# Mixers and norms of a hybrid encoder: sums of squares from split values, decay projection and meta keys on 128 rows, low parts of the gate weights on VectorE

## The chip, the cores and the metric

The kernel runs on one core of a Trainium2 chip. The metric is device time in microseconds (us) of one execution; three runs of the kernel before took 2300.5, 2293.67 and 2294.09, a median of 2294.09. The engines are called as in the profile: PE is TensorE's matmuls and PEld its weight loads, DVE is VectorE, ACT is ScalarE, POOL is GpSimd, SP is SyncE, which only issues transfers here.

## The reference, cut to what matters

A trunk of two layers works on 528 tokens (512 and 16 meta tokens) of 1024 channels, in float32. Each layer is half a feed-forward network, a mixer and another half feed-forward network, each behind an RMS norm.

```python
for l in range(2):
    h = h + 0.5 * swiglu(rmsnorm(h, g[l, 0]), ...)      # 1024 -> 2816 -> 1024
    h = h + mixer(rmsnorm(h, g[l, 1]), ...)
    h = h + 0.5 * swiglu(rmsnorm(h, g[l, 2]), ...)
out = rmsnorm(h, final_norm)[:, 16:]                    # without the meta tokens

rmsnorm(x, g) = x * rsqrt(mean(x * x) + 1e-6) * g

mixer(z):
    q_a, k_a, v_a, r_a, lr_f, lr_b, q_b, k_b, v_b, g_a, g_b = split(z @ w_in)
    a = gla_branch(...)         # 4 heads; decay = log_sigmoid(lr @ w2 + b2) / 16, lr of rank 16,
                                # one decay for each of two directions; heads normed, times silu(r_a)
    b = attention_branch(...)   # 8 query heads of 64, 2 key/value heads, q and k normed and rotated
    return (sigmoid(g_a + b0) * (a @ w_pa) + sigmoid(g_b + b1) * (b @ w_pb)) @ w_out
```

## The kernel before

Activations lie transposed: channels on the 128 partitions, tokens along the row, in two halves of 264 tokens. TensorE multiplies float32 in two ways. A plain float32 matmul passes over its rows several times. Everything large is split instead: a value is the sum of a high part, rounded to a faster type (fp32r in the profile) by a ScalarE copy, and a low part, the rest, by a VectorE subtraction; a product is then three fp32r matmuls, high by high, high by low and low by high (`product`, L374 to L383, the matmul in L382).

*Weights.* Slabs of 128x1024 arrive in the order of a plan, on SP's queue, up to six ahead (class `Weights`). `make` (L210 to L231) turns a slab into its two parts, up to four ahead: ScalarE casts it (`whi`, L222) and VectorE subtracts (`wlo`, L227). For the last twelve gate projections of a mixer, which TensorE works on beside attention, a flag `by_dma` chooses another way to the low part: ScalarE writes the negated high part (L224), and a transfer issued by GpSimd adds the slab to it (L225, by way of L178).

*Feed-forward networks* (L482 to L574) build seven products in place of eight by sums of weight blocks; their matmul is L502 and the change leaves them alone, but their norms are the `Norm` below.

*Norms.* `Norm` collects the squares of the channel chunks in a float32 tile (L414 to L420). `rs` (L458) has TensorE add them over the partitions, with a constant matrix of 1/1024 in float32 (`means`, L385 to L389), and `rsqrt_of` (L391) takes the root with a logarithm, an exponential and one correction step. The norms of the linear attention's heads (L735 to L737) and of the attention's keys (L759) use `means` with matrices of 1/128 and 1/64. The last norm stands in the tail (L1005 to L1025), in two column halves.

*The mixer* (L916 to L971) loads the decay weights `w2t` (33 rows: two times 16 ranks and a bias, L921), projects r, takes the norm's root, projects the low-rank values (`product` with 32 columns, L933; a row of ones is added, L935) and then runs `gla_pair` for two pairs of heads. In `gla_pair`, for each direction, L612 multiplies `w2t` with `lr` on 33 rows in float32, VectorE and ScalarE make the cumulated decays of it, and the keys times decay are transposed (L655). Then come the states of four blocks of 128 tokens and the meta tokens (L691 to L711), the scores (L718), and the outputs, from the scores (L727) and from the state (L728). A state has the forward direction on partitions 0 to 63 and the backward one on 64 to 127; block 3, the last, has no backward state and the meta block no forward one, so there L728 uses 64 rows.

*Attention* (L752 to L906). `probs` makes the softmax of 128 queries: two times two score matmuls, a maximum on VectorE, an exponential on ScalarE, a normalisation. `weighted` (L853 to L880) transposes the probabilities of two such blocks (L861), splits them, and multiplies them with the values. The values are stored as high part in 64 columns and low part in the next 64, so one matmul with the probabilities' high part (L878) and one with their low part (L879) give all products. The 16 meta keys come last, as a contraction over 16 rows of `vm` (L772) and `tail`. For each of the two key heads there are eight sums of 256 columns in each layer, and in layer 0 one of 64 columns for the meta tokens' own queries: 34 in all.

*The order.* The program is written for a scheduler that decides each engine's order from dependencies and priorities; `tc.high_priority` marks the work behind a norm's sum. Each engine then takes its instructions in that order. Tiles come from pools with a fixed number of buffers (six of `t`, one of `lr` in the mixer), and a write waits until the buffer's last reader is through.

```python
if self.by_dma:                                                                   # L223
    nc.scalar.activation(lo[:, cs], hi[:, cs].bitcast(F32), AF.Copy, scale=-1.0)  # L224
    self.add(lo[:, cs].bitcast(F32), w[:, cs])                                    # L225
else:
    nc.vector.tensor_tensor(lo[:, cs], w[:, cs], hi[:, cs].bitcast(F32), ALU.subtract)
```

Of the kernel before, what the change touches and what calls it, by code (L numbers as in the profile page):

```python
# [17 lines left out]
P = 128  # L18
D = 1024
# [8 lines left out]
EPS = 1e-6  # L28
NB = SEQ // P
# [107 lines left out]
C_O1024, C_O128, C_B64 = C_ID + P, C_ID + 2 * P, C_ID + 3 * P  # L137
C_DIAG = C_ID + 4 * P
NCONST = C_DIAG + P


class Weights:
# [3 lines left out]
    def __init__(self, nc, raw, hi, lo, wts, win):  # L146
        self.nc, self.raw, self.hi_pool, self.lo_pool, self.wts, self.win = nc, raw, hi, lo, wts, win
        self.long = self.short = None
        self.by_dma = False
# [59 lines left out]
    def make(self, upto):  # L209
        nc = self.nc  # L210
        while self.made < min(upto, len(self.loads)):
# [8 lines left out]
            for a in np.split(np.arange(SLAB), 2 if s == 0 else 1):  # L220
                cs = slice(a[0], a[-1] + 1)
                nc.scalar.copy(hi[:, cs], w[:, cs])  # L222
                if self.by_dma:  # L223
                    nc.scalar.activation(lo[:, cs], hi[:, cs].bitcast(F32), AF.Copy, scale=-1.0)  # L224
                    self.add(lo[:, cs].bitcast(F32), w[:, cs])  # L225
                else:
                    nc.vector.tensor_tensor(lo[:, cs], w[:, cs], hi[:, cs].bitcast(F32), ALU.subtract)  # L227
# [11 lines left out]
    def next(self, name):  # L239
# [5 lines left out]
        return hi[:, c : c + t[5]], lo[:, c : c + t[5]]  # L245

# [7 lines left out]
def build(tc, ctx, xt, wts, win, par, w2, const, umask, out):  # L254
# [70 lines left out]
    o1024, o128 = ct[:, C_O1024 : C_O1024 + P], ct[:, C_O128 : C_O128 + P]  # L325
# [59 lines left out]
    def means(weights, x):  # L385
        acc = Acc("ss", x.shape[-1])
        for a, hs in zip(acc.half, acc.spans):
            TE.matmul(a, weights, x[:, hs], start=True, stop=True)  # L388
        return acc  # L389

    def rsqrt_of(acc, y, newton):  # L391

        (ms, cut), = acc.parts
        S.activation(cut(y), ms, AF.Ln, bias=eps, scale=1.0)
        act(y, y, AF.Exp, scale=-0.5)
        if newton:
            u = slot("t", n=y.shape[-1])
            S.activation(u, y, AF.Square)
            V.scalar_tensor_tensor(cut(u), ms, EPS, cut(u), ALU.add, ALU.mult)
            V.scalar_tensor_tensor(y, u, 3.0, y, ALU.subtract, ALU.mult)  # L400

    class Norm:
# [55 lines left out]
        def rs(self):  # L458

            rs = slot("rs")  # L460
            with tc.high_priority():
                ms = means(o1024, self.acc)
                with after(table("natural_log_exp_and_others")):
                    rsqrt_of(ms, rs, True)
# [125 lines left out]
    def gla_pair(l, p, lr, w2t, sr, qa, ka, va, n_out):  # L590
# [17 lines left out]
        for d in range(2):  # L608
            z = pair()
            for i, hs in enumerate(halves):  # L610
                c0 = p * 256 + d * P
                TE.matmul(z[:, i, :HF], w2t[:33, c0 : c0 + P], lr[:33, hs], start=True, stop=True)  # L612
# [61 lines left out]
        st_m = slot("k")  # L674

# [34 lines left out]
        for b in [3, 2, 1, 0] + [NB] * (n_out == T):  # L710
# [383 lines left out]
```

## Time and profile before

| | before |
|---|---|
| three runs, us | 2293.67, 2294.09, 2300.5 |
| median, us | 2294.09 |
| the profiled execution's span, us | 2289.1 |
| weights and activations read | 264.38 MB, 116 GB/s over the span |
| L382, split products in the mixers, x6570 | 494.2 + 383.5 + 309.9 + 267.2 us busy in its four largest groups |
| L502, split products of the feed-forward networks, x7392 | 902.3 + 702.1 us busy |
| L227, low parts of weights on VectorE | 267.9 + 203.1 + 107.6 us busy |

The span is that of the profiled execution, from its first to its last instruction; the runs are timed without a profile. Busy time of TensorE is modelled from the start and the length of its matmuls: two that follow each other 0.12 us apart can each be recorded with 0.28 us, since a matmul's length holds the time until its result has left the array. What a matmul costs the queue is therefore read from start to start.

The page cuts the span into 40 slices of 57 us. Layer 0's mixer lies between some 390 and 806 us, layer 1's between some 1535 and 1930 us; TensorE is at 9 tenths or more in all slices but the first, the 21st and the last.

### The profile page before, as it was taken

The page shows a single profiled execution, that of the slowest core. Times are in us where ns is not written, and L with a number is a line of the kernel's source. Part 1 is how long each engine was busy: PE and PEld are TensorE (multiplying, and loading weights), DVE is VectorE, ACT ScalarE, POOL GpSimd, SP SyncE. Part 2 cuts the span into 40 slices and gives each one's busy share as a digit, 9 for nine tenths or more (in the row PEclk, how much of TensorE's full clock was granted, in tenths as well). Part 3 has the DMA queues.
Part 4 walks back from the last instruction along what each step waited for, and adds up shares of the span by engine and source line. Part 5 has one row for each costly group of instructions (what it writes and reads, how often), then busy time and mean ns, then how long its engine had stood idle before and what let it go on. Part 6 is the DMA issues. An engine that isn't in the chain of part 4 may idle for free.

```text
span 2289.1 us, 39919 instructions
## 1 busy us (share of the span) xinstructions
PE 2225.1 (97%) x16548; PEld 2108.4 (92%) x16548; DVE 1491.3 (65%) x2355; ACT 1214.4 (53%) x1785; POOL 195.1 (9%) x218
## 2 busy tenths in 40 slices
PE   5999999999999999999989999999999999999997
PEld 5999999989999999999989999998788888989896
DVE  6656567476775676565676565674768667756566
ACT  7536355344786564453565353553448946636452
POOL 1111010010000010101011110100000001101010
PEclk9999999999999999999989999999999999999999
DMA  8858562211325485766667585632113356859661
GB/s 225 236 150 224 142 175 93 74 57 56 84 56 157 117 214 153 189 180 173 181 141 202 151 219 146 170 98 74 56 65 93 74 156 152 223 149 223 159 176 61
DMA packets 91869, 327.79 MB, mean 143 GB/s; under 512 B 10214, under 2 KB 12646, under 8 KB 91688
## 3 DMA queue, kind: packets, MB, share of 16 engines
q1 hardware_dynamic: 61136, 218.26, 28.7%
q0 software_dynamic: 28800, 104.87, 25.6%
q8 instruction: 130, 2.13, 0.4%
q10 hardware_dynamic: 1752, 2.11, 0.3%
q14 instruction: 51, 0.42, 0.1%
HBM read 264.38 MB, written 2.10 MB: 116 GB/s over the span
## 4 chain that ended last, share of the span: by engine, by line
PE 89%; DVE 5%; DMA 2%; ACT 2%; issue 1%; SPq 0%; DVEq 0%; POOL 0%; ACTq 0%
PE ss L502 36%; PE ss L382 27%; PE mm L382 14%; PE sm L382 3%; PE sm L861 1%; PE sm L878 1%; DVE wlo L227 1%; PE sm L879 1%; PE ss L836 1%; DMA w<-win 1%; PE ss L837 1%; PE ss L388 1%; DMA s<-win 1%; PE ss L718 1%; DMA w<-s 1%
## 5 line engine op out<-in xcount | busy, mean ns | idle before, releaser
L502 PE MATMUL ss<-xc,whi 128*128 128x264 f32 (+1 forms) x4928 | 902.3, 285 | 26.5 <-ACT snap L508 9.7
L502 PEld LDWEIGHTS ss<-xc,whi 128*128 128x128 f32 x4928 | 766.8, 189 | 29.3 <-ACT snap L508 10.3
L502 PE MATMUL ss<-xc,wlo 128*128 128x264 f32 (+1 forms) x2464 | 702.1, 285 | 4.3 <-DVE wlo L227 4.3
L382 PE MATMUL ss<-g,whi 128*128 128x264 f32 (+2 forms) x2668 | 494.2, 301 | 0.0
L502 PEld LDWEIGHTS ss<-xc,wlo 128*128 128x128 f32 x2464 | 466.0, 189 | 5.3 <-DVE wlo L227 5.1
L382 PEld LDWEIGHTS ss<-g,whi 128*128 128x128 f32 x2668 | 388.6, 188 | 17.4
L382 PE MATMUL mm<-x,whi 128*128 128x264 f32 (+1 forms) x1712 | 383.5, 315 | 0.0
L222 ACT CAST whi<-w 128x1024 fp32r<-128x1024 f32 (+1 forms) x221 | 230.8, 1047 | 263.1 <-PE ss L382 118.7
L222 ACT CAST whi<-raw 128x1024 fp32r<-128x1024 f32 x190 | 199.3, 1049 | 299.5 <-PE mm L382 106.9
L227 DVE TENSOR_TENSOR wlo<-w,whi 128x1024 fp32r<-128x1024 f32 (+1 forms) x221 | 267.9, 1218 | 110.7 <-ACT whi L222 108.4
L382 PE MATMUL ss<-g,wlo 128*128 128x264 f32 (+2 forms) x1334 | 309.9, 301 | 0.0
L382 PEld LDWEIGHTS mm<-x,whi 128*128 128x128 f32 x1712 | 279.5, 189 | 18.8 <-issue 2.1
L382 PE MATMUL mm<-x,wlo 128*128 128x264 f32 (+1 forms) x856 | 267.2, 317 | 0.0
L227 DVE TENSOR_TENSOR wlo<-raw,whi 128x1024 fp32r<-128x1024 f32 x166 | 203.1, 1224 | 95.2 <-ACT whi L222 94.2
L382 PEld LDWEIGHTS ss<-g,wlo 128*128 128x128 f32 x1334 | 213.4, 188 | 8.7
L227 DVE TENSOR_TENSOR wlo<-s,whi 128x1024 fp32r<-128x1024 f32 x88 | 107.6, 1223 | 102.0 <-ACT whi L222 101.9
L222 ACT CAST whi<-s 128x1024 fp32r<-128x1024 f32 x88 | 92.4, 1050 | 153.6 <-PE ss L502 135.4
L382 PEld LDWEIGHTS mm<-x,wlo 128*128 128x128 f32 x856 | 160.4, 189 | 10.8 <-issue 2.2
L469 DVE SCALAR_TENSOR_TENSOR t<-ss,rs 128x528 f32<-128x528 f32 (+1 forms) x95 | 66.0, 700 | 127.8 <-PE ss L382 127.7
L173 ACT ACTIVATE s<-w 128x1024 f32<-128x1024 f32 x88 | 93.3, 1060 | 79.2 <-DMA w<-win 41.5
L178 POOL DMA_DIRECT2D s<-win x44 | 40.8, 927 | 497.0 <-ACT s L173 489.2
L508 ACT COPY snap<-ss 128x528 f32<-128x528 f32 (+1 forms) x132 | 77.2, 585 | 0.0
(235 smaller groups left out, 2660.3 us busy)
## 6 DMA issues: line engine op xcount, KB each, us to landing
w<-win SPq DMA_DIRECT2D x219, 512.0 KB, 4.7
raw<-wts SPq DMA_DIRECT2D x190, 512.0 KB, 3.4
s<-win POOLq DMA_DIRECT2D x44, 512.0 KB, 6.8
w<-s POOLq DMA_DIRECT2D x44, 512.0 KB, 5.5
w<-win POOLq DMA_DIRECT2D x44, 512.0 KB, 7.1
s<-w POOLq DMA_DIRECT2D x44, 512.0 KB, 7.4
wlo<-raw POOLq DMA_DIRECT2D x24, 512.0 KB, 4.4
h<-xt SPq DMA_DIRECT2D x3, 528.0 KB, 7.1
```

Of the source, the lines that this page charges most:

```text
L173: self.nc.scalar.activation(t, w, AF.Copy, scale=-1.0)
L178: self.nc.gpsimd.dma_start(t, src, accum_op=ALU.add)
L222: nc.scalar.copy(hi[:, cs], w[:, cs])
L227: nc.vector.tensor_tensor(lo[:, cs], w[:, cs], hi[:, cs].bitcast(F32), ALU.subtract)
L382: TE.matmul(acc.half[i][:width], lhs, rhs[:, acc.spans[i]], start=first, stop=last)
L388: TE.matmul(a, weights, x[:, hs], start=True, stop=True)
L469: V.scalar_tensor_tensor(cut(dst[rows]), pv[rows], -0.5 * f, cut(rs[rows]), ALU.mult, ALU.mult)
L502: TE.matmul(acc[:, j], a[:, j, k], b[:, at], start=bool(begin and k == 0 and i == 0), stop=k == len(x) - 1 and i == 2, skip_group_check=no ...
L508: S.copy(st[name], acc)
L718: TE.matmul(ats[:n, hh, d * n : (d + 1) * n], prods[d][1][rows, bs], prods[d][0][rows, bs], start=True, stop=True)
L836: TE.matmul(s[:n, i, :HF], lhs, kh[:, hs], start=True, stop=False)
L837: TE.matmul(s[:n, i, :HF], lhs, kl[:, hs], start=False, stop=True)
```

## The change: what it does

**Sums of squares from split values.** `totals` (and `split_totals` in the tail) replaces `means`: ScalarE casts the collected squares to a high part, VectorE subtracts the low part, and TensorE adds both with a matrix of ones in fp32r (`whole`, or `ones64` for blocks of 64 rows, both made at the start by ScalarE). The division by the number of channels moves into the scale of the logarithm and of the correction. Two constant matrices of float32 go, and with them a separate load on SP's queue at the start.

**Decay projection.** `w2` is padded to 128 rows on the host: three copies of the 32 rank rows, two bias rows, and zeros. `decay_weights` loads it from ScalarE's queue and makes, row by row, a high part or a low part of it. `low_rank` lays the high and the low part of the low-rank weights side by side, 64 columns, so that two matmuls per chunk and half stand in place of three; it adds the two halves of the result and stores `lr` as high part, low part and high part again, with ones below. The product over 128 rows is then the split product in one matmul of fp32r.

**Meta keys.** `vm` and the tails get 128 rows: rows 0 to 15 the high part of the probabilities, rows 32 to 47 the low part, zeros elsewhere, and the values in both places. One matmul over 128 rows does what two over 16 did. The tails are two halves of one tile that is zeroed once per attention.

**Linear attention.** The missing halves of the states of block 3 and of the meta block are filled with zeros, and L728 always uses 128 rows. The loop over the scores has its two levels exchanged.

**Gate weights.** `by_dma` goes: all low parts of weights are VectorE subtractions.

```diff
-                if self.by_dma:
-                    nc.scalar.activation(lo[:, cs], hi[:, cs].bitcast(F32), AF.Copy, scale=-1.0)
-                    self.add(lo[:, cs].bitcast(F32), w[:, cs])
-                else:
-                    nc.vector.tensor_tensor(lo[:, cs], w[:, cs], hi[:, cs].bitcast(F32), ALU.subtract)
+                nc.vector.tensor_tensor(lo[:, cs], w[:, cs], hi[:, cs].bitcast(F32), ALU.subtract)
...
+    def run(self, name, n):          # the slices of n tiles of the plan that lie in one slab
+        t, (s, c) = PLAN[self.pos], divmod(COLUMN[self.pos], SLAB)
+        self.pos += n
+        return [w[:, c : c + n * t[5]].rearrange("p (k m) -> p k m", k=n) for w in self.use(self.at[s])]
...
-        S.dma_start(ct[:, :C_O1024], const[:, :C_O1024])
-        S.dma_start(ct[:, C_O1024 + P :], const[:, C_O1024 + P :])
+        S.dma_start(ct, const)
         S.dma_start(mask, umask)
+        S.activation(ones64, b64, AF.Copy, scale=float(HD))
...
-    def means(weights, x):
-        acc = Acc("ss", x.shape[-1])
-        for a, hs in zip(acc.half, acc.spans):
-            TE.matmul(a, weights, x[:, hs], start=True, stop=True)
+    def totals(weights, x):
+        n = x.shape[-1]
+        hi, lo = slot("t", F32R, n), slot("t", F32R, n)
+        S.copy(hi, x)
+        V.tensor_tensor(lo, x, hi.bitcast(F32), ALU.subtract)
+        acc = Acc("ss", n)
+        for b, first in ((hi, True), (lo, False)):
+            for a, hs in zip(acc.half, acc.spans):
+                TE.matmul(a, weights, b[:, hs], start=first, stop=not first)
...
-                ms = means(o1024, self.acc)
+                ms = totals(whole, self.acc)
...
-                TE.matmul(z[:, i, :HF], w2t[:33, c0 : c0 + P], lr[:33, hs], start=True, stop=True)
+                TE.matmul(z[:, i, :HF], w2t[:, c0 : c0 + P], lr[:, hs], start=True, stop=True)
...
+        S.activation(st[1][HD:P, 256:512], ct[HD:P, :256], AF.Copy, scale=0.0)
+        S.activation(st_m[0:HD, 0:256], ct[0:HD, :256], AF.Copy, scale=0.0)
...
-            for hh in range(2):
-                rows = slice(hh * HD, (hh + 1) * HD)
-                for d in range(2):
+            for d in range(2):
+                for hh in range(2):
+                    rows = slice(hh * HD, (hh + 1) * HD)
                     TE.matmul(ats[:n, hh, d * n : (d + 1) * n], prods[d][1][rows, bs], prods[d][0][rows, bs],
...
-                rows = slice(0, P) if b < NB - 1 else (slice(0, HD) if b == NB - 1 else slice(HD, P))
-                TE.matmul(os_, state(b)[rows, hh], qin[hh][rows, bs], start=False, stop=True)
+                TE.matmul(os_, state(b)[:, hh], qin[hh][:, bs], start=False, stop=True)
...
-                tail = slot("lr", F32R)
-                hi, lo = tail[:META, :256], tail[:META, 256:512]
-                S.copy(hi[:, :w], tp[:META, :w])
-                V.tensor_tensor(lo[:, :w], tp[:META, :w], hi[:, :w].bitcast(F32), ALU.subtract)
-                parts.append((vs[g][1], hi[:, :w], lo[:, :w]))
+                tail = tails[:, turn[0] * 256 : turn[0] * 256 + w]
+                turn[0] = 1 - turn[0]
+                S.copy(tail[:META], tp[:META, :w])
+                V.tensor_tensor(tail[32 : 32 + META], tp[:META, :w], tail[:META].bitcast(F32), ALU.subtract)
                 for i, (vw, ph, pl) in enumerate(parts):
                     TE.matmul(o[:, :w], vw, ph, start=i == 0, stop=False)
-                    TE.matmul(o[:, :w], vw, pl, start=False, stop=i == len(parts) - 1)
+                    TE.matmul(o[:, :w], vw, pl, start=False, stop=False)
+                TE.matmul(o[:, :w], vs[g][1], tail, start=False, stop=True)
...
+    def decay_weights(l):
+        w, low = slot("t")[:, :512], slot("t")[:, :512]
+        wt = one.tile([P, 512], F32R, tag="w2", name=nm("w2"))
+        S.dma_start(w, w2[l])
+        S.copy(wt, w)
+        V.tensor_tensor(low, w, wt.bitcast(F32), ALU.subtract)
+        S.activation(w, wt.bitcast(F32), AF.Copy, scale=ct[:, C_PICK : C_PICK + 1])
+        V.scalar_tensor_tensor(wt, low, ct[:, C_PICK + 1 : C_PICK + 2], w, ALU.mult, ALU.add)
+        return wt
+
+    def low_rank(x, rs):
+        cols = slot("t", F32R, 2 * RANKS * KC).rearrange("p (k m) -> p k m", k=KC)
+        for i, w in enumerate(W.run("w_in", KC)):
+            (V.tensor_copy if i else S.copy)(cols[:, :, i * RANKS : (i + 1) * RANKS], w.bitcast(F32))
+        acc = Acc("sm")
+        for k, (xh, xl) in enumerate(x):
+            for j, b in enumerate((xh, xl)):
+                for a, cs in zip(acc.half, acc.spans):
+                    TE.matmul(a[: 2 * RANKS], cols[:, k], b[:, cs], start=k == 0 and j == 0, stop=k == KC - 1 and j == 1)
+        lr, u, v = slot("lr", F32R), slot("t"), slot("t")
+        scaled(u, acc, rs, 1.0, slice(0, 2 * RANKS))
+        V.tensor_copy(v[:RANKS], u[RANKS : 2 * RANKS])
+        V.tensor_tensor(u[:RANKS], u[:RANKS], v[:RANKS], ALU.add)
+        S.copy(lr[:RANKS], u[:RANKS])
+        V.tensor_tensor(lr[RANKS : 2 * RANKS], u[:RANKS], lr[:RANKS].bitcast(F32), ALU.subtract)
+        S.copy(lr[2 * RANKS : 3 * RANKS], u[:RANKS])
+        S.activation(lr[3 * RANKS :], ct[3 * RANKS :, :T], AF.Copy, scale=0.0, bias=1.0)
+        return lr
...
-        w2t = one.tile([33, 512], F32, tag="w2", name=nm("w2"))
-        S.dma_start(w2t, w2[l])
+        w2t = decay_weights(l)
...
-        lr = slot("lr")
-        ps = product("w_in", Acc("sm"), x, KC, width=32)
-        scaled(lr, ps, rs, 1.0, slice(0, 32))
-        V.memset(lr[32:33], 1.0)
+        lr = low_rank(x, rs)
...
-        W.by_dma = True
         gates += [project(x, None, "g", n=n_out) for _ in range(2 * KC - EARLY)]
-        W.by_dma = False
...
-        TE.matmul(ms, o1024, fin.acc[:, hs], start=True, stop=True)
+        split_totals(ms, fin.acc[:, hs])
```

Three places show how the order of the instructions moves. In each row stands the line, the operation, the tile that it writes, the tiles that it reads, and the shape; the names are the pools' with a running number, so they differ between the two programs.

The first is TensorE's queue at the end of one weighted sum of layer 0's attention, before: `q` are the split probabilities, `k` the values, `lr` the tail of the meta keys, and the last row is a transpose for the next sum.

```order
L878 MATMUL sm_6334<-q_6330,k_5954 128x256
L879 MATMUL sm_6334<-q_6331,k_5954 128x256
L878 MATMUL sm_6334<-lr_6337,vm_5955 128x256
L879 MATMUL sm_6334<-lr_6337,vm_5955 128x256
L861 MATMUL sm_6376<-const,t_6311 128x128
```

The same place now:

```order
L899 MATMUL sm_6388<-q_6384,k_6002 128x256
L900 MATMUL sm_6388<-q_6385,k_6002 128x256
L901 MATMUL sm_6388<-lr_6018,vm_6003 128x256
L386 MATMUL mm_7469<-x_4052,whi_6082 128x264
L883 MATMUL sm_6437<-const,t_6353 128x128
```

One matmul with `vm` stands where two were, and a matmul of a gate projection (L386, before L382) has come between it and the next transposes.

The second is ScalarE's queue at the start of layer 0's mixer, before: the last chunk's normed operand and square, a cast of weights, and then the norm's logarithm (L394) and exponential (L365).

```order
L410 ACTIVATE x_4272<-h,par 128x528
L416 ACTIVATE t_4276<-h 128x528
L222 CAST whi_4367<-raw_4184 128x1024
L394 ACTIVATE rs_4477<-ss_4478,eps 128x528
L365 ACTIVATE rs_4477<-rs_4477 128x528
```

Now:

```order
L426 ACTIVATE x_4280<-h,par 128x528
L432 ACTIVATE t_4284<-h 128x528
L942 DMA t_4316<-w 128x512
L222 CAST whi_4381<-raw_4192 128x1024
L943 CAST w_4318<-t_4316 128x512
L392 CAST t_4492<-t_4013 128x528
L945 ACTIVATE t_4316<-w_4318,const 128x512
L410 ACTIVATE rs_4491<-ss_4496,eps 128x528
```

The load of the decay weights (L942) is issued behind the last square, and two of the three instructions that came in, the cast of those weights (L943) and the cast of the squares (L392), stand ahead of the norm's sum in that order.

The third is TensorE's queue at the same time: L382 are the projections of r, L388 is the norm's sum, before.

```order
L382 MATMUL ss_4310<-x_4273,whi_4074 128x264 x2
L382 MATMUL ss_4310<-x_4272,wlo_4075 128x264 x2
L382 MATMUL sm_4366<-x_4044,wlo_4128 128x264
L388 MATMUL ss_4478<-t_4005,const 128x264 x2
L382 MATMUL sm_4365<-x_4066,whi_4127 128x264
```

Now, where the sum is L397:

```order
L386 MATMUL sm_4379<-x_4233,wlo_4136 128x264
L397 MATMUL ss_4496<-t_4492,whole 128x264 x2
L386 MATMUL sm_4380<-x_4233,wlo_4136 128x264
L386 MATMUL sm_4379<-x_4280,whi_4135 128x264
L386 MATMUL sm_4380<-x_4280,whi_4135 128x264
L397 MATMUL ss_4496<-t_4493,whole 128x264 x2
```

The sum has become two pairs of matmuls, for the high and for the low part, and stands 24 and 28 rows later in the queue, behind the projection of the next r tile.

More of the change, by code (lines that the diff above doesn't have):

```diff
@@ L28 @@
 EPS = 1e-6
+RANKS = 32
 NB = SEQ // P
@@ L245, in next @@
         return hi[:, c : c + t[5]], lo[:, c : c + t[5]]
+    def run(self, name, n):
+        t, (s, c) = PLAN[self.pos], divmod(COLUMN[self.pos], SLAB)
+        assert all(u[1] == name and u[5] == t[5] for u in PLAN[self.pos : self.pos + n]) and c + n * t[5] <= SLAB
+        self.pos += n
+        return [w[:, c : c + n * t[5]].rearrange("p (k m) -> p k m", k=n) for w in self.use(self.at[s])]
     def op(self, *load):
@@ L324, in build @@
     ident = ct[:, C_ID : C_ID + P]
-    o1024, o128 = ct[:, C_O1024 : C_O1024 + P], ct[:, C_O128 : C_O128 + P]
+    whole, ones64 = [one.tile([P, P], F32R, name=n) for n in ("whole", "ones64")]
+    S.activation(whole, eps.broadcast_to([P, P]), AF.Copy, scale=0.0, bias=1.0)
     b64, diag2 = ct[:, C_B64 : C_B64 + P], ct[:, C_DIAG : C_DIAG + P]
@@ L989, in build @@
     W.fetch(2)
-    nc.sync.dma_start(ct[:, C_O1024 : C_O1024 + P], const[:, C_O1024 : C_O1024 + P])
     for c in range(KC):
@@ L1076 @@
     par[:, G_FIN:] = a["final_norm"].reshape(-1, P).T
-    w2 = np.zeros((DEPTH, 33, 512), np.float32)
+    w2 = np.zeros((DEPTH, P, 512), np.float32)
     for p in range(2):
```

53 lines of the change are left out of this document (32 added, 21 removed).

## The prediction

> **What bounds the kernel now.** I read the page's busy shares first, then the chain of work that ended last.
>
> ```profile
> PE 2225.1 (97%) x16548; PEld 2108.4 (92%) x16548; DVE 1491.3 (65%) x2355; ACT 1214.4 (53%) x1785; POOL 195.1 (9%) x218
> PE 89%; DVE 5%; DMA 2%; ACT 2%; issue 1%; SPq 0%; DVEq 0%; POOL 0%; ACTq 0%
> ```
>
> TensorE is busy for 2225 of 2289 us and makes 89% of the chain. So the first question for every edit is what it does to TensorE's time, the second whether TensorE gets a new wait. Attention is where that could be false, since it hangs on long chains through VectorE and ScalarE. The chain in order of time answers:
>
> ```profile
> 697.39 16.21 PE mm L382 x132
> ```
>
> Right behind layer 0's last attention matmul TensorE still has 132 matmuls of gate projections, 16.2 us. Gate projections fill the holes of attention, and some are left when it ends: attention is not late, TensorE is. Time taken from TensorE in the mixer therefore shortens the layer. The waits that remain in the mixer stand in the list of waits:
>
> ```profile
> PE ss L655 <- DVE p L651: 11.8, 8, 2.0
> ```
>
> Eight times, TensorE waits some 1.5 us for the decay chain of linear attention.
>
> **What leaves TensorE.** A matmul's own duration holds its latency, so I count from start to start in the timeline. First the meta keys, at the end of one weighted sum (start, length, line, operation, rows*columns of the array):
>
> ```profile
> 586.78 0.28 PE L878 MATMUL sm<-q,k 128*128 128x256 f32 x1
> 586.90 0.28 PE L879 MATMUL sm<-q,k 128*128 128x256 f32 x1
> 587.11 0.38 PE L878 MATMUL sm<-lr,vm 16*128 16x256 f32 x1
> 587.33 0.27 PE L879 MATMUL sm<-lr,vm 16*128 16x256 f32 x1
> 587.54 0.33 PE L861 MATMUL sm<-const,t 128*128 128x128 f32 x1
> ```
>
> Matmuls on 128 rows follow each other every 0.12 us. At the change to 16 rows the step is 0.21, the next is 0.22, and the change back costs 0.21: 0.64 us for three matmuls. The change puts both into one matmul of 128 rows, so two steps remain, 0.24. That is 0.40 us in each of 34 sums:
>
> ```profile
> L878 PE MATMUL sm<-lr,vm 16*128 16x256 f32 x32 | 12.2, 381 | 0.0
> L878 PE MATMUL sm<-lr,vm 16*128 16x64 f32 x2 | 0.6, 294 | 0.0
> ```
>
> 34 x 0.40 = **13.6 us**. The decay projection works on 33 rows in plain float32:
>
> ```profile
> 439.57 0.28 PE L382 MATMUL mm<-x,whi 128*128 128x264 f32 x1
> 439.88 1.15 PE L612 MATMUL ss<-lr,w 33*128 33x264 f32 x4
> 440.96 0.39 PE L382 MATMUL mm<-x,wlo 128*128 128x264 f32 x1
> 441.19 0.29 PE L382 MATMUL mm<-x,whi 128*128 128x264 f32 x1
> ```
>
> Two float32 matmuls stand in the trace as four pieces. From 439.57 to 441.19 are 1.62 us, of which two ordinary steps are 0.24: the block costs 1.38. Afterwards it is two matmuls of the split type on 128 rows, 0.24. Eight blocks (four pair calls, two directions) save 8 x 1.14 = **9.1 us**.
>
> The sums of squares are float32 on 128 rows, so here the type alone counts:
>
> ```profile
> 392.97 1.05 PE L388 MATMUL ss<-t,const 128*128 128x264 f32 x4
> 393.98 0.53 PE L382 MATMUL sm<-x,whi 128*128 128x264 f32 x3
> ...
> L388 PE MATMUL ss<-t,const 128*128 128x264 f32 x44 | 13.9, 443 | 4.1 <-DVE t L420 4.1
> L388 PE MATMUL ss<-t,const 128*128 128x512 f32 x10 | 5.6, 644 | 1.3 <-DVE t L420 1.3
> ```
>
> 1.01 us between these starts hold the four pieces and one ordinary step: 0.89. Four split matmuls (high and low part, two halves) take 0.48, so 0.41 goes; 44 pieces are 11 sums, 4.5 us. The five sums of 512 columns save 0.39 each by their width, 2.0. Together **6.5 us**.
>
> The low-rank projection runs 48 matmuls of 32 weight columns:
>
> ```profile
> 409.27 0.65 PE L382 MATMUL sm<-x,whi 128*32 128x264 f32 x4
> ...
> 415.07 0.41 PE L382 MATMUL mm<-x,whi 128*128 128x264 f32 x2
> ```
>
> 5.80 us for 48 is 0.121 each, the pace of 128 columns; fewer columns buy nothing. High and low weights side by side leave 32 matmuls, and two layers save 32 x 0.121 = **3.9 us**. Last, the state of block 3, used on 64 rows:
>
> ```profile
> 473.54 0.49 PE L727 MATMUL sm<-t,q 128*128 128x128 f32 x2
> 473.96 0.49 PE L728 MATMUL sm<-p,q 64*128 64x128 f32 x2
> ...
> 475.54 0.39 PE L728 MATMUL sm<-p,q 128*128 128x128 f32 x2
> 475.76 0.39 PE L727 MATMUL sm<-t,q 128*128 128x128 f32 x2
> ```
>
> The eight pieces up to 475.54 alternate between 128 and 64 rows and take 2.00 us; on 128 rows two take 0.22, so eight take 0.9 and one change stays: 1.0 saved, four times, **4.0 us**. For the reordered loop over L718 I take nothing:
>
> ```profile
> 470.56 0.71 PE L718 MATMUL ss<-p,p 64*128 64x128 f32 x6
> 471.20 0.71 PE L691 MATMUL sm<-q,q 128*128 128x128 f32 x4
> ```
>
> Six pieces pass in the time of four, since the upper and lower 64 rows work side by side already; new order, same pieces.
>
> Sum: 13.6 + 9.1 + 6.5 + 3.9 + 4.0 = **37.1 us less on TensorE**, and nothing that it gains.
>
> [...]
>
> **What is added.** *VectorE in attention.* The low parts of 24 gate slabs were made by a ScalarE pass and an accumulating transfer, and now by a VectorE subtraction:
>
> ```profile
> L224 ACT ACTIVATE wlo<-whi 128x1024 fp32r<-128x1024 f32 x24 | 25.5, 1062 | 0.2
> L227 DVE TENSOR_TENSOR wlo<-raw,whi 128x1024 fp32r<-128x1024 f32 x166 | 203.1, 1224 | 95.2 <-ACT whi L222 94.2
> 590.00:640.00 50.00, 49.66 (x373) 46.31 (x372) 41.38 (x110) 40.42 (x85) 3.48 (x4) 0.97 0.30 76
> 640.00:700.00 60.00, 59.92 (x457) 54.88 (x456) 36.82 (x97) 52.27 (x111) 3.44 (x4) 1.00 0.32 78
> ```
>
> VectorE gains 24 x 1.22 = 29.4 us, ScalarE loses 25.5. The windows (TensorE, weight loads, VectorE, ScalarE) show VectorE at 83% in the middle of attention and 61% after it, where ScalarE is the fuller one at 87%. Slabs are made four ahead and VectorE has room over the stage, but its queue is in order: what stands behind a subtraction, the maxima of the softmax and the low parts of the probabilities, comes 1.2 us later, and TensorE waits for those. Bounds: nothing (ScalarE's relief even helps) to all 29.4. I take 3, near the lower end, because of the gate matmuls left over.
>
> *Start of the mixer.* The padded decay weights are 256 KB, loaded from ScalarE's queue just before they are needed; behind the load wait, in ScalarE's order, a cast of them, then the cast for the sum of squares, on which TensorE waits.
>
> ```profile
> 391.25 0.63 ACT L416 ACTIVATE t<-h 128x528 f32<-128x528 f32 x1
> out<-h ACTq DMA_DIRECT2D x4, 256.0 KB, 2.3
> w<-win SPq DMA_DIRECT2D x2, 256.0 KB, 5.3
> ```
>
> Issued after the last square ends at 391.9, the load lands at 394.2 by the first transfer row, or 397.2 by the second, which fell among the start's other loads. Two half-microsecond casts later the sum's high part exists, at 395.3 or 398.3. The sum now stands 24 matmuls later on TensorE: 392.97 + 23 x 0.12 = 395.7. So the wait is 0 to 2.6 us, plus the low part's subtraction behind it; I take 1 per layer, **2 us**.
>
> *Other norms and the tail.* A sum now waits for a cast and a subtraction more.
>
> ```profile
> L433 ACT CAST xc<-t 128x528 fp32r<-128x528 f32 x24 | 14.8, 621 | 2.5 <-DVE t L445 1.6 <-DVE t L442 0.9
> 2276.98 0.42 DVE L1013 TENSOR_TENSOR t<-t,t 128x256 f32<-128x256 f32 x1
> 2277.45 1.02 PE L1016 MATMUL ss<-t,const 128*128 128x256 f32 x2 [2.31 <-DVE t L1013]
> ```
>
> 0.62 for a cast, 0.70 for a full-width VectorE pass as the chain's L420: at most 1.3 at each of four other norms, 5.3; the program has moved their sums behind 8 to 12 more matmuls, so I take 1. In the tail nothing hides 0.4 + 0.4, and the two halves' matmul gets shorter: 0.5. *Linear attention*: zero fills on ScalarE lengthen the chain of the eight waits, at most 8 x 0.4 by a 264-column cast's 402 ns, while more gate matmuls now stand ahead of L655, which could take up to the 11.8 us: 0. *Start*: one load less, and GpSimd issues its second and third transfer in the other order, ahead of
>
> ```profile
> 23.97 7.41 DMA w<-win
> ```
>
> for which TensorE waits until 33 us; 2 us either way, taken as 0.
>
> Sum of the added: 3 + 2 + 1 + 0.5 = 6.5. Net 37.1 - 6.5 = **30.6 us less**. The profiled span is 2289.1, 5 us under the median of 2294.1 of the runs; I take the difference from the median: **2263.5 us**.
>
> **Rivals.** *VectorE becomes the bound of attention*: for it the 83% window, which four more slabs would bring to 93%; against it ScalarE's relief and the leftover gate matmuls. If two thirds of the 29.4 are exposed in place of 3, the time is 2263.5 + 17 = 2280, up to 2290 for all. *A long wait at the mixer's start halves the clock*:
>
> ```profile
> 1170.17 0.78 PE L502 MATMUL ss<-xc,whi 128*128 128x264 f32 x2 [7.34 <-ACT xc L433]
> 1170.97 0.64 PE L502 MATMUL ss<-xc,whi 128*128 128x264 f32 x2
> ```
>
> After 7.3 us of idle time the matmuls step by 0.22 us in place of 0.12, for some 8 us. If the late load makes such a wait in both layers, each costs 3 more of wait and 4 of slow matmuls: 2277. [...] *The row count is not what costs the steps* (it would be the operands' recent arrival, say): then keys save only one matmul each, 34 x 0.12 = 4.1, state none, decay only its type, 8 x 0.65 = 5.2: a sum of 19.7 less 6.5, 2281. Against it, the 128-row pieces of L728 and L727 alternate at full pace with other weights each time. *Slower*: VectorE's queue in the mixer carries 29.4 us of subtractions, 16 low parts of sums at 0.70 (11.2), and behind ScalarE's 16 casts at 0.62 (9.9): 50.5. All of it in TensorE's order would give 37.1 - 50.5, 13 us slower, 2307; it decides once more than 44 us are exposed.
>
> **How the numbers follow.** Forecast, 2249 to 2276: 0.68. VectorE bound: 0.16, a third of it within 0.3% of before. Clock: 0.07. Row count: 0.04. Slower: 0.05. The low end takes in half of the eight waits vanishing (6), the start's 2 and attention's 3 and the norms' 3, the high end most of the VectorE case: **2249 to 2284**. A measurement tells about 0.3%, 6.9 us, from no change: faster 0.90, same 0.05, slower 0.05.
>
> **What would show it.** Right: one vm matmul per sum at a 0.12 us step; the decay block at 0.24; two sums of squares where four pieces were; TensorE busy near 2188 us; gate matmuls still left behind attention. Wrong: TensorE waiting for the VectorE operations of the softmax, a ScalarE queue standing at the decay weights' cast with TensorE idle for over 2 us, or halved clock there.

## The result and the profile after

The changed kernel took 2269.89 us, median of four runs (2266.95 to 2273.16), beside 2295.72 us of the kernel before in the same comparison (a fourth run of it, 2297.34, moved its median from the 2294.09 that the forecast started from). The ratio is 0.9887, 95% interval 0.9868 to 0.9905: 25.8 us less, where 30.6 were forecast; the time lies inside the stated range. The profiled execution spans 2266.1 us, 23.0 less than before. First the page of the kernel after: busy time by engine, and the chain that ended last.

```profile
PE 2196.9 (97%) x16466; PEld 2094.4 (92%) x16466; DVE 1537.0 (68%) x2411; ACT 1211.1 (53%) x1807; POOL 173.7 (8%) x194
PE 88%; DVE 5%; ACT 4%; DMA 2%; issue 1%; SPq 0%; DVEq 0%; ACTq 0%
```

TensorE is 28 us less busy (2197 us, where near 2188 was forecast) and still 97% of the span. So the change did what it says, and the bound is the same engine. What the list of TensorE's waits shows is new (total, times, longest):

```profile
PE ss L671 <- DVE p L667: 13.7, 8, 2.3
...
PE ss L404 <- ACT t L402: 5.1, 2, 2.7
...
PE ss L405 <- DVE t L403: 3.2, 1, 3.2
```

L671 is the old L655: its eight waits grew from 11.8 to 13.7 us. L404 and L405 are the high and the low part of the tail's two sums; now TensorE waits 8.3 us there. Before, it waited 4.3:

```profile
PE ss L1016 <- DVE t L1013: 4.3, 2, 2.3
```

Next the timeline at the end of one weighted sum, and at the first decay block.

```profile
581.70 0.29 PE L900 MATMUL sm<-q,k 128*128 128x256 f32 x1
581.82 0.28 PE L901 MATMUL sm<-lr,vm 128*128 128x256 f32 x1
581.93 0.28 PE L386 MATMUL mm<-x,whi 128*128 128x264 f32 x1
...
436.68 0.28 PE L386 MATMUL mm<-x,whi 128*128 128x264 f32 x1
436.98 0.51 PE L628 MATMUL ss<-lr,w 128*128 128x264 f32 x2
437.33 0.28 PE L386 MATMUL mm<-x,wlo 128*128 128x264 f32 x1
437.45 0.41 PE L386 MATMUL mm<-x,whi 128*128 128x264 f32 x2
```

One matmul for the meta keys steps by 0.12 us, as forecast. Counted as in the prediction, from the matmul ahead to the second start behind, less two ordinary steps, this decay block costs 0.53 us where 0.24 was forecast. It is the dearest one: the eight average 0.33 (an ordinary step is 0.22 where the neighbour has 512 columns). Its first matmul starts 0.30 us behind the one ahead and steps by 0.23. Many sums of squares also begin with a long step:

```profile
480.87 0.28 PE L386 MATMUL mm<-x,whi 128*128 128x264 f32 x1
481.12 0.51 PE L397 MATMUL ss<-t,whole 128*128 128x264 f32 x2
481.48 0.28 PE L386 MATMUL mm<-x,whi 128*128 128x264 f32 x1
```

The matmul ahead steps by 0.25 and the pair takes 0.36 in place of 0.24. Of the 19 pairs of 264 columns that ran at full clock, 12 begin with a step of 0.17 to 0.23 us; it comes where the operand has just been written. In all 12 the write (L392 or L393) ended at most 0.11 us before the matmul's start, in the other seven at least 0.15 us. The forecast had taken 0.12 for all.

At the start of layer 0's mixer TensorE waits for nothing: the load of the decay weights was issued at 390.01 us, ahead of the last square, and ScalarE's casts follow each other.

```profile
390.01 0.34 ACTq L942 DMA_DIRECT2D t<-w  x1
...
392.21 1.05 ACT L222 CAST whi<-raw 128x1024 fp32r<-128x1024 f32 x1 [0.94 <-PE ss L386]
393.17 0.61 ACT L943 CAST w<-t 128x512 fp32r<-128x512 f32 x1
393.69 0.63 ACT L392 CAST t<-t 128x528 fp32r<-128x528 f32 x1
```

Last, linear attention in layer 1: the timeline behind one of the waits, and the windows around it (TensorE, weight loads, VectorE, ScalarE, GpSimd busy; granted clock; DMA).

```profile
1641.85 0.63 PE L671 MATMUL ss<-const,p 128*128 128x128 f32 x4 [1.83 <-DVE p L667]
...
1643.79 0.42 PE L386 MATMUL mm<-x,wlo 128*128 128x264 f32 x1
1644.01 0.64 PE L386 MATMUL mm<-x,whi 128*128 128x264 f32 x2
1644.45 0.42 PE L386 MATMUL mm<-x,wlo 128*128 128x264 f32 x1
...
1630.00:1642.00 12.00, 10.17 (x63) 8.92 (x62) 11.10 (x23) 6.81 (x12) 1.73 (x1) 1.00 0.25 87
1642.00:1654.00 12.00, 12.00 (x65) 10.30 (x65) 7.31 (x19) 2.78 (x6) 0.00 (x0) 0.57 0.13 45
1654.00:1666.00 12.00, 12.00 (x94) 11.11 (x93) 6.92 (x16) 6.65 (x16) 0.00 (x0) 1.00 0.01 1
```

Behind a wait of 1.83 us matmuls step by 0.22 us: the clock is halved for 10.2 us (the mean granted clock of the middle window is 0.57). This was forecast for the mixer's start, not for here.

### The profile page after: what moved, and what is told of

Its sections match the earlier page's. It is cut to its first block, busy times and chain, and to the rows that moved or that the text cites. A ratio compares the mean times of both kernels' runs of the same rounds, so it can differ in the third digit from the quotient of the medians.

```text
span 2266.1 us, 39764 instructions
## 1 busy us (share of the span) xinstructions
PE 2196.9 (97%) x16466; PEld 2094.4 (92%) x16466; DVE 1537.0 (68%) x2411; ACT 1211.1 (53%) x1807; POOL 173.7 (8%) x194
## 4 chain that ended last, share of the span: by engine, by line
PE 88%; DVE 5%; ACT 4%; DMA 2%; issue 1%; SPq 0%; DVEq 0%; ACTq 0%
PE ss L518 37%; PE ss L386 27%; PE mm L386 13%; PE sm L386 2%; PE sm L883 1%; PE ss L858 1%; DVE wlo L223 1%; PE sm L899 1%; DMA s<-win 1%; PE ss L859 1%; PE sm L709 1%; PE sm L900 1%; DMA w<-s 1%; ACT whi L222 1%; PE ss L736 1%
## 5 line engine op out<-in xcount | busy, mean ns | idle before, releaser
L518 PE MATMUL ss<-xc,whi 128*128 128x264 f32 (+1 forms) x4928 | 903.8, 285 | 30.6 <-ACT xc L449 12.3
L386 PE MATMUL ss<-g,whi 128*128 128x264 f32 (+2 forms) x2668 | 494.1, 301 | 0.0
L386 PEld LDWEIGHTS ss<-g,whi 128*128 128x128 f32 x2668 | 388.6, 188 | 17.1
L386 PE MATMUL mm<-x,whi 128*128 128x264 f32 (+1 forms) x1712 | 385.1, 315 | 0.0
L223 DVE TENSOR_TENSOR wlo<-w,whi 128x1024 fp32r<-128x1024 f32 (+1 forms) x221 | 267.8, 1218 | 106.2 <-ACT whi L222 103.1
L386 PE MATMUL ss<-g,wlo 128*128 128x264 f32 (+2 forms) x1334 | 310.1, 301 | 0.0
L223 DVE TENSOR_TENSOR wlo<-raw,whi 128x1024 fp32r<-128x1024 f32 x190 | 232.1, 1222 | 104.4 <-ACT whi L222 103.6
L386 PEld LDWEIGHTS mm<-x,whi 128*128 128x128 f32 x1712 | 280.6, 190 | 15.6 <-issue 0.4
L386 PE MATMUL mm<-x,wlo 128*128 128x264 f32 (+1 forms) x856 | 264.5, 314 | 0.0
L386 PEld LDWEIGHTS ss<-g,wlo 128*128 128x128 f32 x1334 | 213.5, 188 | 8.7
L223 DVE TENSOR_TENSOR wlo<-s,whi 128x1024 fp32r<-128x1024 f32 x88 | 107.6, 1223 | 101.5 <-ACT whi L222 101.5
L386 PEld LDWEIGHTS mm<-x,wlo 128*128 128x128 f32 x856 | 161.1, 190 | 7.4
L178 POOL DMA_DIRECT2D w<-win x44 | 38.6, 878 | 591.1 <-DVE g L1008 204.4
```

Of the source, the lines that this page charges most:

```text
L178: self.nc.gpsimd.dma_start(t, src, accum_op=ALU.add)
L386: TE.matmul(acc.half[i][:width], lhs, rhs[:, acc.spans[i]], start=first, stop=last)
L518: TE.matmul(acc[:, j], a[:, j, k], b[:, at], start=bool(begin and k == 0 and i == 0), stop=k == len(x) - 1 and i == 2, skip_group_check=no ...
```

## How the experiments are read

Single runs of one kernel differ by up to 11 us, and they follow the mean granted clock: the nine runs of the changed kernel took 2265.5 to 2268.1 us at 0.988 and 0.989, 2271.8 and 2273.2 at 0.987, 2273.6 and 2276.3 at 0.986 and 0.985. Which stretches run at half clock thus moves a median by several us, as much as some edits. Where the same stretches run at half clock, as in after and again, the stages repeat to 0.1 us (mixers 796.6 and 796.6, tail 19.7 and 19.7). So the table gives, beside the runs, the **mixers**: the time from the first r projection to the first matmul of the next feed-forward network, both layers added, by the starts in the trace; the time in them with a granted clock of 0.5; and the mixers less half of that time, an estimate of what they take at full clock. Traces with the same mixers and other stretches (again and tail_f32, ke_first and ke_tail) differ by 0.5 and 0.7 us in that estimate, so less than 1 us there says nothing. The tail runs from the start of the last down projection matmul to the end of the span.

| kernel | median us | ratio to before, 95% interval | mixers | half clock | mixers at full clock | tail |
|---|---|---|---|---|---|---|
| before | 2295.72 | | 820.2 | 6.8 | 816.8 | 16.9 |
| after | 2269.89 | 0.9887 [0.9868, 0.9905] | 796.6 | 17.1 | 788.0 | 19.7 |
| again | 2268.11 | 0.9895 [0.9877, 0.9913] | 796.6 | 17.1 | 788.0 | 19.7 |
| keys_64 | 2272.63 | 0.9902 [0.9887, 0.9917] | 804.1 | 20.5 | 793.9 | 19.7 |
| tail_f32 | 2267.85 | 0.9885 [0.9870, 0.9899] | 801.1 | 27.3 | 787.5 | 16.6 |
| low_by_dma | 2269.49 | 0.9891 [0.9877, 0.9904] | 798.7 | 20.5 | 788.5 | 19.7 |
| old_keys | 2277.09 | 0.9920 [0.9896, 0.9944] | 807.1 | 20.5 | 796.9 | 19.7 |
| old_decay | 2274.91 | 0.9913 [0.9887, 0.9938] | 803.8 | 10.2 | 798.7 | 19.7 |
| old_sums | 2270.48 | 0.9902 [0.9877, 0.9928] | 798.6 | 13.7 | 791.7 | 19.7 |
| old_gla | 2270.56 | 0.9896 [0.9866, 0.9926] | 792.6 | 3.4 | 790.9 | 20.0 |
| ke_first | 2261.63 | 0.9873 [0.9856, 0.9890] | 784.1 | 0.0 | 784.1 | 19.8 |
| ke_tail | 2257.22 | 0.9849 [0.9834, 0.9864] | 786.8 | 6.8 | 783.4 | 16.9 |

The first three edits ran beside "again" on one chip, the four "old" ones on a second, the last two on a third, each with runs of the kernel before on that chip (medians 2294.18, 2294.09, 2292.51).

## The experiments

All edits start from the changed kernel.

**again**: the changed kernel once more.

> The changed kernel itself, as the base of this series. Expected as in the first result: about 25.8 us less than before, a ratio of 0.987 to 0.991, a span of 2265 to 2271. If single executions differ by which stretches of linear attention run at the halved clock, this trace has such stretches at other places than the first one (462 and 1643 us), and the spans differ by some 5 us; if the stretches belong to the program, they stand at the same places.

2268.11 us, and the same stretches at half clock: 461.5 and 1642.5 us. That alone does not tie them to the program: tail_f32, which differs in the tail alone, has 13.7 us of it at 517 us, where these two have none, and old_keys, the same up to attention, has 13.7 us at 516 us and none in layer 1: the execution has a part in it too.

**keys_64**: the meta keys' matmul on 64 rows in place of 128.

```diff
-                TE.matmul(o[:, :w], vs[g][1], tail, start=False, stop=True)
+                TE.matmul(o[:, :w], vs[g][1][:HD], tail[:HD], start=False, stop=True)
```

> The matmul of the meta keys takes rows 0 to 63 of the same tiles; the rows that it leaves out hold zeros. Theory: a change of the number of rows costs the steps, so L901 steps by 0.21 us and the matmul behind it starts 0.2 us later than now, 34 x 0.18 = 6 us more on TensorE and 5 to 6 us in the time, since gate matmuls stand ready behind. Rival: what cost the time before was the operand that had just arrived, or the second matmul; then one matmul on 64 rows costs what one on 128 does, and the time stays within 1 us of the changed kernel.

The timeline at the sum shown above:

```profile
583.30 0.28 PE L900 MATMUL sm<-q,k 128*128 128x256 f32 x1
583.51 0.38 PE L901 MATMUL sm<-lr,vm 64*128 64x256 f32 x1
583.82 0.39 PE L386 MATMUL mm<-x,whi 128*128 128x264 f32 x1
```

The step to the matmul is 0.21 us and the one behind it 0.31, with the same operands and half the rows. The mixers take 5.9 us longer at full clock (6 expected). The row count is the cause; the rival falls. That the size fits so well is in part luck: from the matmul ahead to the one behind a sum now takes 0.52 us in place of 0.24, which makes 9.2 us over the 34 sums, 6 of them expected, and about a third of it does not reach the mixers' time, as in old_keys below.

**tail_f32**: the tail's sums as plain float32 matmuls.

```diff
-        split_totals(ms, fin.acc[:, hs])
+        TE.matmul(ms, whole.bitcast(F32), fin.acc[:, hs], start=True, stop=True)
```

> The two sums in the tail as one plain float32 matmul each again, all else as in the changed kernel. Theory: in the changed tail the second half's subtraction stands behind the first half's five products on VectorE (3.35 us), so this gives back 2.5 us of waiting and 0.8 us of cast and subtraction: the stretch from the end of the last down projection to the end of the span goes from 19.6 to about 16.5 us, and the time is 3 us lower than the changed kernel's. Rival: the tail is longer because its matmuls run at the halved clock; then float32 pieces at that clock cost 0.4 us each and the stretch stays within 1 us of 19.6.

The tail goes from 19.7 to 16.6 us, 3.1 less, while it still runs at half clock. In the changed kernel's timeline the reason is VectorE's queue:

```profile
2252.73 3.35 DVE L1069 TENSOR_TENSOR h<-h,t 128x256 f32<-128x256 f32 x5
...
2256.00 0.41 DVE L403 TENSOR_TENSOR t<-t,t 128x256 fp32r<-128x256 f32 x1
2256.47 0.58 PE L405 MATMUL ss<-t,whole 128*128 128x256 f32 x1 [3.18 <-DVE t L403]
```

The cast for the second half was done at 2252.65, but its subtraction stands behind the first half's five products. The runs' median, expected 3 us lower, is that of "again" within its spread. A likely reason is the clock: in this kernel's trace 13.7 us at half clock came up at 517 us.

**low_by_dma**: the gate slabs' low parts by ScalarE and the accumulating transfer again (the `by_dma` lines of the diff put back).

> The low parts of the 24 gate slabs by ScalarE and an accumulating transfer again, all else as in the changed kernel. Theory of the forecast: VectorE's 29.4 us of subtractions cost attention 3 us, so this is 3 us faster than the changed kernel. Rival: gate matmuls cover all of VectorE's delays, so the time stays within 1 us, and only the idle time of VectorE and ScalarE moves. A second rival: ScalarE's relief helps attention, so this is slower by 2 us or more, with TensorE waiting longer for exponentials.

The mixers take 0.5 us more at full clock, which that estimate cannot tell from nothing, and the median agrees with "again" within its interval. The windows of attention show that the work moved and TensorE was as busy; first the changed kernel, then this one:

```profile
590.00:640.00 50.00, 49.86 (x398) 47.33 (x397) 46.21 (x112) 38.20 (x87) 0.00 (x0) 1.00 0.16 54
```

```profile
590.00:640.00 50.00, 49.47 (x389) 46.47 (x388) 43.72 (x114) 41.96 (x92) 3.47 (x4) 1.00 0.35 85
```

VectorE is at 92% with the subtractions, as the forecast's rival had computed (93%), and TensorE is idle for 0.14 of 50 us. The rival of VectorE as the bound falls, and so do the 3 us.

**old_keys**: two matmuls on 16 rows (the meta-key lines of the diff undone).

> The meta keys again as two matmuls on 16 rows, all else as in the changed kernel. Theory: the whole term of the forecast comes back, 13.2 us by the steps of the two traces (13.6 forecast), in the stretches from the first score to the first matmul of the next network: 229.6 us in layer 0 and 212.9 in layer 1 become 442.5 + 13 together. Rival: attention's chains through VectorE and ScalarE hide part of it, and under 8 us come back.

8.9 us come back at full clock, between the two expectations. The steps at the sums themselves differ by 13.2 us between the traces. Layer 0 has 6.8 of these, but its stretch from the first score to the next network differs by 3.9 only. A likely reason is that TensorE, where keys cost less, more often meets probabilities that have just been written. In layer 0 the steps from a gate matmul to a transpose exceed the plain step by 2.8 us in sum in the changed kernel and by 0.9 here, those to a score matmul by 2.0 and 1.1: 2.8 of the missing 2.9. In layer 1 the same steps explain 0.7 of 1.9 missing, so a part stays open.

**old_decay**: the decay projection on 33 rows in float32, and the low-rank projection with 32 columns (both undone).

> The decay projection on 33 rows in plain float32 and the low-rank projection with 32 columns again, all else as in the changed kernel. Theory: the low-rank part gives 1.9 us a layer back between the first r matmul and the first decay matmul; of the 7 us of the decay matmuls themselves only some 4 show, since TensorE's waits for the decay chain (13.7 us now, 11.8 before) shrink when it has more to do in between: 8 us in all. Rival: the waits do not depend on TensorE's work, and 11 us come back. Forecast terms: 3.9 + 9.1 = 13.0.

10.7 us come back at full clock: nearer to the rival's 11 than to the 8 of the theory. 2.1 us a layer are the low-rank part. The eight waits did shrink, to 10.8 us, without giving back what the theory had put on them.

**old_sums**: float32 sums in all norms but the last.

```diff
-        hi, lo = slot("t", F32R, n), slot("t", F32R, n)
-        S.copy(hi, x)
-        V.tensor_tensor(lo, x, hi.bitcast(F32), ALU.subtract)
...
+            TE.matmul(a, weights.bitcast(F32), x[:, hs], start=True, stop=True)
```

> The sums of squares of all norms but the last as plain float32 matmuls again, without the cast and the subtraction, all else as in the changed kernel. Theory: the first matmul of each pair that follows a fresh operand steps by 0.226 us in place of 0.12, and so the sums save 3.7 us on TensorE in place of 6.5; with the cast and the subtraction gone the heads' and the norms' chains get 1.1 to 1.3 us shorter each, so this costs 2 us or less, and may be faster. Rival, the forecast: 6.5 less 1 of waits, 5.5 us slower than the changed kernel.

3.7 us come back at full clock, between the two. The split sums are worth it in the mixers, with two thirds of what was forecast.

**old_gla**: states on 64 rows, old loop order, no zero fills (undone).

> Block 3's and the meta block's states on 64 rows, the scores' loop in its former order, no zero fills on ScalarE; all else as in the changed kernel. Theory of the forecast: 4.0 us slower, all of it in the outputs (L744 and L745), nothing for the order of the scores and nothing for the fills. Rival: the fills or the new order of the scores lengthen the chain or bring the halved clock (461 and 1642 us in the changed kernel), and undoing them gives back 2 us or more: the waits for the transposed keys (13.7 us) fall below 12, and the stretches at half clock in linear attention are gone.

2.9 us come back at full clock (4.0 forecast). In this trace only 3.4 us of half clock were left, so its span of 2262.6 is even shorter than the changed kernel's; but its four runs lie between 2264.4 and 2276.3, as far apart as the changed kernel's, and the waits are 13.0 us. So the fills and the loop order neither make the waits nor settle the clock.

**ke_first**: in `gla_pair` the exponential that the keys need and their product come ahead of the others (for the first direction; the second alike):

```diff
+            with tc.high_priority():
+                    V.tensor_tensor(blk(ct_), blk(src), tot, ALU.subtract)
+                    V.tensor_tensor(ct_[:, MB], src[:, MB], mm_, ALU.subtract)
+                    S.activation(ct_, ct_, AF.Exp, scale=-r16)
+                V.tensor_tensor(ke, ka, eend, ALU.mult)
...
-            ke = slot("p")
-            V.tensor_tensor(ke, ka, eend, ALU.mult)
```

> The changed kernel with one chain put in another order: in linear attention the exponential that the keys' product needs is made first and the product (L667 of the changed kernel) second, before the other exponentials, the queries' product and the copies of the decays; same instructions, same numbers. Theory: TensorE's eight waits (13.6 us) are the order on VectorE and ScalarE, where L667 stands 2 to 3 us behind the first exponential, so the product comes some 3 us earlier, while the scheduler puts the transposes 5 to 15 matmuls (0.6 to 1.8 us) earlier: 4 us of waits at most remain, the stretches at half clock in linear attention go with them, and the time falls by 8 to 12 us against the changed kernel. Rival: the scheduler, which places the transposes as early as it believes them ready, takes up all of the gain; the waits stay over 10 us and the time within 2 us of the changed kernel's.

The wait list of this kernel (its L679 is the transpose, L661 and L664 what it waits for):

```profile
PE ss L679 <- DVE p L661: 5.5, 7, 1.4
```

With 0.5 us more on L664, 6.0 us are left of 13.6 (4 at most were expected); 2.1 us of new waits for GpSimd's product have come, which is now late. No stretch of the mixers ran at half clock. The mixers are 12.5 us shorter than in "again", 3.9 at full clock. The runs' median is 6.5 us lower, where 8 to 12 were expected, on a chip where the kernel before ran 1.7 us faster, and their spread, 2256.2 to 2266.2, is still wide. The waits were in large part the order, as the theory had it; its size was not reached, and the rival (waits over 10 us) falls.

**ke_tail**: ke_first and tail_f32 together.

> The same, and the two sums of the tail in plain float32 as in tail_f32. Theory: the two add up, 3.0 us less than ke_first in the stretch from the last down projection to the end (16.7 in place of 19.7 us) and the same as ke_first elsewhere; 11 to 15 us less than the changed kernel. Rival: the half clock, which falls elsewhere in each program, takes the 3 us back in the runs' median.

2257.22 us: 10.9 less than "again" (11 to 15 expected), and a ratio of 0.9849 [0.9834, 0.9864]. It beats both kernels; its interval lies below the changed kernel's. The tail's gain of 2.9 us stands beside ke_first's.

## Why the prediction held, and which steps did not

The forecast was 30.6 us, the measurement 25.8, interval 21.8 to 30.3 by the ratio. In the profiles the mixers took 23.6 us less (820.2 to 796.6), the tail 2.8 more and the rest some 2 less, together the 23.0 of the spans. The terms:

| step of the prediction | forecast us | by the steps of the two traces | undone, at full clock |
|---|---|---|---|
| meta keys | -13.6 | -13.2 | -8.9 |
| decay and low rank | -13.0 | -11.9 | -10.7 |
| sums of squares | -6.5 | -3.7 | -3.7 |
| block 3's state | -4.0 | -3.4 | -2.9 |
| VectorE in attention | +3 | | -0.5 |
| start of the mixers | +2 | 0 | |
| other norms | +1 | in the sums | |
| tail | +0.5 | +2.8 | +3.1 |
| eight waits of linear attention | 0 | +1.9 | |
| half clock in the mixers | 0 | +5.1 (17.1 less 6.8 us, halved) | |

Undone one at a time, the edits in the mixers give back 26.7 of the 28.8 us by which the mixers shorten at full clock; half clock takes back 5.1. That the sum came within 5 us of the forecast is in part luck: 5 us were taken for costs that did not come (VectorE and the mixers' start), and half clock and the tail cost 7.4 us that were not in it.

**What leaves TensorE** was right in mechanism. Row changes cost what the steps showed (keys_64: 0.21 us into the matmul, 0.31 out of it), and the 32 weight columns of before stepped by 0.121 us, no less than 128: the low-rank part came out at its 3.9. What was too small is the price after. For the new matmuls the step of an undisturbed stream, 0.12, was used, where the first of a pair often takes up to 0.23. In the sums that is the one whose operand has just been written, and it makes most of their missing 2.8 us. The decay blocks cost 0.33 us in place of 0.24, and before 1.32 (the seven at full clock) in place of the first one's 1.38. Their operand had long been written (`lr` at 415.6 us, the first block at 436.98), so why they step slowly stays open. For the keys the step was right, and what was missing is that a third of the steps saved does not shorten attention.

**VectorE in attention** was the wrong reason for a loss that exists. The subtractions cost nothing that the runs can tell (low_by_dma). But of the keys' 13.2 us some 4 are given back in attention, likely in longer steps behind fresh probabilities (old_keys), and that is about what the term held. The cover named in the forecast, the gate matmuls left over, is there: right behind layer 0's attention stood 132 of them before, 16.2 us, and now 101:

```profile
690.34 12.33 PE mm L386 x101
```

**The tail** is the step that failed by most for its size, 0.5 us forecast and 2.8 measured: "nothing hides 0.4 + 0.4" counted the two instructions and not the queue in which the second one stands. VectorE's order was weighed for attention and for the mixer's start, not here.

**The clock** was put at the wrong place. The rival had a long wait at the mixer's start, which did not come. Half clock came in linear attention, behind waits that were there before. The 7.3 us of the forecast are not the only place in the trace of before: there the clock is halved also for 3.4 us from 591.5 us, where TensorE waits for nothing, and for 3.4 us from 1642.8 us, behind a wait of 1.66 us. So in these traces the length of a wait does not tell whether half clock follows: after the change a wait of 1.83 us stands ahead of 10.2 us at half clock, while one of 2.30 us at 515 us in the same trace was followed by none.

What tells the two waits apart can be counted in the traces. From 60 us on, the stretches of the changed kernel's trace start at 462.41, 585.29, 1155.31, 1165.55, 1643.42 and 2250.99 us: 36, 203, 206, 346 and 524 times 3.413 us behind the first. Divide the trace into pieces of 3.413 us, from 462.41 both ways. The wait of 1.83 us (1640.02 to 1641.85) lies inside one piece, the one that ends where the half clock begins. The wait of 2.30 us (512.84 to 515.14) crosses a boundary, at 513.6. In the first piece TensorE began matmuls of 2192 columns in sum, in the later piece of the second wait 2720; the median piece has 7392. In the traces of before and after, each divided so and counted from 60 us on, every piece at full clock with fewer than 2300 columns was followed by half clock (8 of 8), of those with 2300 to 3000 columns 2 of 9, and of the 1261 with more none. So in these two traces the columns that TensorE begins in a piece go with the clock behind it much more closely than the length of a wait. This is a count over two traces; no run changed it on purpose, and why the clock is halved was not shown. Of the two kernels in which these waits are shorter (6.0 us in ke_first, 13.6 in the changed kernel), ke_first has no stretch in the mixers and ke_tail one of 3.4 us in linear attention.

## What to carry to other kernels

On an engine that works through a queue, price an inserted instruction by what stands ahead of it on that queue at that moment, not by its own length; the tail's 0.4 us became 3 that way. Where a few matmuls in an otherwise full stream use another row count, pad them to the stream's: here the step into such a matmul took 0.21 us and the step out of it 0.21 to 0.31, in place of 0.12. When an edit is worth less than one per cent, compare stages of traces and the runs' granted clock beside the medians.

## What the runs showed of the hardware

From 60 us on, the stretches at half clock in the traces of before and after last 3.4, 6.8, 10.2 or 13.7 us, apart from the one that runs into the end, and within each trace they start whole multiples of 3.413 us apart (168, 308 and 494 times behind the first in that of before).

VectorE's product for the keys took longer where it lay beside GpSimd's product of the same shape: L667 took 1.71 us at 459.72 us, while L665 ran on GpSimd from 459.02 for 1.85. In the traces of before and after three of these 16 products overlap GpSimd's and take 1.34 to 1.72 us; the other 13 take 0.69 to 0.71. A weight subtraction (L223, at 443.76 us) that lay beside GpSimd's product for 0.87 of its time took 1.22 us, as the median one does, and so did the four others in the two traces that lay beside it for 0.93 us or more; one in the trace of before, at 448.05 us and beside it for 0.45 us, took 1.53. Both stretches at half clock in the changed kernel's linear attention stand behind such a long L667 (459.72 and 1640.37 us, the latter 1.34 us long). Why these products took longer was not shown.
